# Moving key, value and chunk products of a hybrid encoder block into its scan, and re-ordering four waiting instructions

## The chip, the cores and the metric

One core of a Trainium2 chip runs the whole kernel in one launch. The metric is the device time of one execution in microseconds (us), as the median of the runs shown.

## The reference, cut to what matters

One layer on x of shape 1024 tokens x 1024 features, float32. A projection `z = rmsnorm(x) @ w_in` (4528 columns) feeds two branches:

```python
q = (rmsnorm(c_q) @ w_uq)                   # 8 heads, 64 plain + 32 rotary
kv = (rmsnorm(c_kv) @ w_ukv)                # 8 heads: k_nope (64), v_a (64)
o_a = softmax attention(q, [k_nope, k_rope], v_a)
q, k, v = silu(conv5(gdn_qkv))              # 4 heads of 128, q and k l2-normalised
o_b = delta rule scan, forward + backward   # state S_t per head, gated by g and beta
merged = sigmoid(gate_a) * (o_a @ w_proj_a) + sigmoid(gate_b) * (o_b @ w_proj_b)
x = x + merged @ w_out
x = x + square(relu(rmsnorm(x) @ w_ff1)) @ w_ff2
return rmsnorm(x)
```

`kv`, the products `q k^T` of the scan's chunks, the first projection, the second feed-forward product and the last norm are the places that the change touches.

## The kernel before, in words

Every matrix product in float32 precision is made of three passes of a reduced float32 form: each operand is split into a high part (a cast by ScalarE, ACT) and a low part (a subtraction by VectorE, DVE), and high x high, high x low and low x high are added up in PSUM (`mm3`, L158). Weights come through `wtile` (L143): a DMA on SyncE's queue (SP) into one of three `wraw` buffers, the cast (L147) and the subtraction (L149) into two of four `ws` buffers. One product with one input tile is 6 matmuls of 128x512. Tiles of 1024 columns come from two pools, `mem` (35 buffers) and `fill` (5 buffers); PSUM has two tiles of 1024 columns (`psA`) and four of 512 (`psB`). Within a program order that is set by the Python code, a list scheduler places each engine's instructions by its own model of the times; on the chip each engine then takes its queue strictly in that order, so an instruction that waits holds everything behind it on its engine.

The stages, with the times of the profiled execution:

- **Start (0 to about 40 us).** SP loads `w_in[0]`, eight tiles of x and, after the fourth, `w_in[1]` (L212 to L217). Each tile of x is scaled and cast on ACT (L233), its low part made on DVE (L234); the casts and low parts of the two weights are `wsplit` (L219; ACT L221, DVE L225), that of `w_in[1]` behind the fifth tile of x (L238). `z_pass` (L256, matmuls L258) goes through the tiles for both weights.
- **Projection stage (to 516 us).** The letters of the string `ORDER` (L45) say in which order the steps are emitted: `g` and `k`, `v`, `q` are tiles of the first projection (48 matmuls each, L156; DVE scales the result, L297), `s` and `i` the triangular solve (POOL masks it at L512, DVE works through it at L551 and L553), `c` the latent norms, `S` transposes, `Q` the attention queries, `z` the solve's products with chunks (transposes L693, L694). `K` (L622) makes keys of two heads: 6 matmuls, a scaled copy on ACT (L628) and a DMA to DRAM from ACT's queue (L629). `V` (L632) makes values of two blocks of 128 tokens: 3 matmuls each (L637), a copy on ACT (L639), a DMA from ACT's queue (L640). The weight of both, `wkv`, is loaded by the first `K`.
- **Chunk products (516 to 523 us).** `KQ` (L746): for four pairs of chunks, 8 products of 128x128 (each two instructions of the profile, L753) and one scaling on DVE (L756).
- **Scan (523 to 614 us).** Eight steps (L966), each for a forward and a backward chunk: `st_k` (L799 on PE, L801 on DVE), `st_v` (L810; DVE L815 makes R, ACT L818 copies vn), `st_s` (L828, DVE L832: the state), `st_o` (L845 with the state, L846 with vn; then ACT L849 or DVE L851). `scan_prep` of the next step is emitted after `st_v`: it loads a decay row (SP, L775, into a tile of `fill`), ACT L777, POOL L779 and L783, ACT L786, DVE L789. Step s uses chunk s forward and 7-s backward, so steps 0 and 1 need the pairs 0 and 3 alone, steps 2 to 5 the pairs 1 and 2. `load_v` reads the values back (SP L947, casts ACT L960, POOL and DVE L961); half of it is emitted in steps 3 and 4.
- **Attention (to 840 us), projections (to 1006 us), first feed-forward product (to 1316 us).** Untouched.
- **Second feed-forward product (1316 to 1591 us).** It begins with eight plain products (`plain_products` L1470: `mm3`, then DVE L1478 adds the result to Y), into which the weights of the first of 15 block products (`Visit`, L1108) are prepared: `blocks` (L1125) makes sums on DVE (L1128 to L1131) of the tiles that `load` (L1118, SP L1122) brings.
- **End (to 1654 us).** Four pieces of 256 tokens: 8 products (`piece` L1534), squares on ACT, sums on POOL and DVE, and `finish` (L1523), which norms the piece before, two of the eight tiles (DVE L1530, SP L1532) for each product of the next piece. The last piece is normed at L1578 to L1591.

Of the kernel before, what the change touches and what calls it, by code (L numbers as in the profile page):

```python
# [20 lines left out]
F32 = mybir.dt.float32  # L21
F32R = mybir.dt.float32r
I32 = mybir.dt.int32
AF = mybir.ActivationFunctionType
ALU = mybir.AluOpType
# [4 lines left out]
D = 1024  # L30
S = 1024
# [4 lines left out]
N = S // C  # L36
# [5 lines left out]

ORDER = "kkkmrvGGklGtvSvvGsciiSigiigcSSgiQigQQiiQgQgQigQgiQqgigoggiKVKVViKgigogigzzqggzqKqzggV"  # L45
PIECES = tuple((i, i + 256) for i in range(0, S, 256))
LEAD, LAG = 3, 2
VS, VS2 = (3, 4), (0, 1)
# [48 lines left out]
def block_kernel(ctx: ExitStack, tc: tile.TileContext, xT, pos, cpar, gpar, w_in, w_uq, w_ukv,  # L97
# [22 lines left out]
    def pb(name):  # L120
        return psB.tile([128, 512], F32, tag="B", name=name)
# [21 lines left out]
    def wtile(src, name):  # L143
        raw = wp.tile([128, 1024], F32, tag="wraw", name=f"{name}_r", bufs=3)
        nc.sync.dma_start(raw, src)
        hi = wp.tile([128, 1024], F32R, tag="ws", name=f"{name}_h", bufs=4)
        A.copy(hi, raw)  # L147
        lo = wp.tile([128, 1024], F32R, tag="ws", name=f"{name}_l", bufs=4)
        V.tensor_tensor(lo, raw, hi.bitcast(F32), ALU.subtract)  # L149
        return hi, lo  # L150
# [62 lines left out]
    for k in range(8):  # L213
        xt.append(mem.alloc())
        nc.sync.dma_start(xt[k].ap, xT[k * 128:(k + 1) * 128, :])
        if k == 3:
            w1 = wraw(w_in[1], "wi1")  # L217

    def wsplit(raw, name):  # L219
# [10 lines left out]
    for k in range(8):  # L230
        h, l = mem.pair()
        for sl in (HS if k < 2 else [slice(0, 1024)]):
            cast = A.activation(h.r[:, sl], xt[k].ap[:, sl], AF.Copy, scale=pcol(N1 + k))  # L233
            V.scalar_tensor_tensor(l.r[:, sl], xt[k].ap[:, sl], pcol(N1 + k), h.ap[:, sl],  # L234
                                   ALU.mult, ALU.subtract)
        xs.append((h, l))
        casts.append(cast)
        if k == 4:  # L238
            early.append(wsplit(w1, "wi1"))
    acc = fill.alloc()  # L240
    for k in range(8):
# [331 lines left out]
    lat = {}  # L573
# [46 lines left out]
                t.free()  # L620

    def s_K(h):  # L622
        if h == 0:
            wts["k"] = wtile(w_ukv, "wkv")
        psk = pa(f"ps_kk{h}")
        mm3(psk, wts["k"], h, [lat[1]])
        t = fill.alloc()
        A.mul(t.ap, psk, math.sqrt(SCALE))  # L628
        A.dma_start(d_k[h], t.ap)  # L629
        t.free()  # L630

    def s_V(i):  # L632
        for kb in (2 * i, 2 * i + 1):
            ks = slice(kb * 128, (kb + 1) * 128)
            psv = pb(f"ps_vv{kb}")
            for j, (a, b) in enumerate(((0, 0), (0, 1), (1, 0))):
                T.matmul(psv, lat[1][a].r[:, ks], wts["k"][b][:, 512:1024], start=j == 0, stop=j == 2)  # L637
            t = half("v")
            A.copy(t, psv)  # L639
            A.dma_start(d_v[kb], t)  # L640
        if i == 3:
            for t in lat[1]:
                t.free()


    d_gc = d_vl[3]
# [72 lines left out]
    def s_q(h):  # L719
# [1 line left out]
        late[0] = conv_tile(qT[h].ap, 12 + h, h)  # L721

    steps = {"k": s_k, "m": s_m, "l": s_l, "r": s_r, "G": s_G, "s": s_s, "t": s_t, "v": s_v,
             "S": s_S, "i": s_i, "g": s_g, "c": s_c, "Q": s_Q, "K": s_K, "V": s_V, "o": s_o,
             "z": s_z, "q": s_q}
    seen = dict.fromkeys(steps, 0)
    for c in ORDER:
# [15 lines left out]
        return lst[h].ap[:, n * C:(n + 1) * C]  # L743


    KQ = []  # L746
    for n2 in range(N // 2):
        psq = pa(f"ps_kq{n2}")
        for n in (2 * n2, 2 * n2 + 1):
            cs = slice(n * C, (n + 1) * C)  # L750
            for h in range(H):
                o = (n % 2) * 512 + h * 128
                T.matmul(psq[:, o:o + 128], kT[h].ap[:, cs], qT[h].ap[:, cs], start=True, stop=True)  # L753
        t = mem.alloc()
        rcol = st[:, i_r, 0:32].rearrange("p (h n) -> p n h", h=H)[:, 2 * n2:2 * n2 + 2, :]
        V.tensor_tensor(t.ap.rearrange("p (n h c) -> p n h c", n=2, h=H),  # L756
                        psq.rearrange("p (n h c) -> p n h c", n=2, h=H),
                        rcol.unsqueeze(3).to_broadcast([128, 2, H, C]), ALU.mult)
        KQ.append(t)


    OT = [mem.alloc().ap for _ in range(H)]
# [202 lines left out]
        scan_prep(0, d)  # L965
    for step in range(N):  # L966
        if step == N - 1:
            for t in KQ[::3] + KST:
                t.free()
        cc = []  # L970
        for d in range(2):
            n = step if d == 0 else N - 1 - step
            cc.append({"key": (step, d, n, slice(n * C, (n + 1) * C),
                               [d * 32 + h * N + n for h in range(H)])})
        for i, f in enumerate((st_k, st_v, st_s, st_o)):
            for c in cc:
                f(c)
            if i == 1 and step + 1 < N:
                for d in range(2):
                    scan_prep(step + 1, d)  # L980
            if i == 3 and step in VS:
                load_v(VS.index(step))
            if i == 3 and step + 2 == N:
                for t in KQ[1:3]:
                    t.free()
                for _ in load_head(0):
                    pass
            if i == 1 and step + 1 == N:
                for qb in range(LEAD):
                    attn_scores(0, qb)  # L990
                spill_q()
# [116 lines left out]
    class Visit:  # L1108


        def __init__(self, name, order, raw, xops, done):
            self.name, self.order, self.raw, self.xops, self.done = name, order, raw, xops, done
            self.g = len(xops)
            self.n = self.g * 128
            self.r = self.sums = self.banks = None
            self.w = {}

        def load(self):  # L1118
# [6 lines left out]
        def blocks(self):  # L1125
            (a11, a21), (a12, a22) = [(t[:, 0], t[:, 1]) for t in self.r]
            s3, s2, s1, s4 = (half(f"s{i}")[:, 0:self.n] for i in (3, 2, 1, 4))
            V.tensor_tensor(s3, a11, a21, ALU.subtract)  # L1128
            V.tensor_tensor(s2, a22, s3, ALU.subtract)
            V.tensor_tensor(s1, a21, a22, ALU.add)  # L1130
            V.tensor_tensor(s4, a12, s2, ALU.subtract)  # L1131
            self.sums = {1: a11, 2: a12, 3: s4, 4: a22, 5: s1, 6: s2, 7: s3}
# [115 lines left out]
    def run(visits, each):  # L1248
        seq = [(v, i) for v in visits for i in v.order]
        ahead = 3  # L1250
        for n in range(-ahead, len(seq)):
            if n + ahead < len(seq):
                v, i = seq[n + ahead]
                q = visits.index(v)
                if v.r is None:
                    v.load()
                if i == v.order[3] and q + 1 < len(visits):
                    visits[q + 1].load()
                v.prep(i)
            if n >= 0:  # L1260
                v, i = seq[n]
                each(v, i)
                v.product(i)
# [206 lines left out]
    def plain_products():  # L1470
        ul = ul0
        for mp in range(4):
            if mp < 3:
                w = wtile(w_ff2t[0, mp], f"w2_{mp}")
            for m in (2 * mp, 2 * mp + 1):
                ps = pa(f"ps_y{m}")
                mm3(ps, w if mp < 3 else [x.r for x in w3], m % 2 * 4, ul)
                V.tensor_tensor(Y[m], ps, Y[m], ALU.add)  # L1478
                if m == 7:
                    for t in w3 + [x for p in ul for x in p]:  # L1480
                        t.free()
                yield

    pp = plain_products()
    for m in range(6):
        next(pp)
# [12 lines left out]
    for q, (_, m, j0, j1) in enumerate(PLAN):  # L1499
        src = w_ff2[m].rearrange("p (a c) -> p a c", a=4)[:, :, j0 * 128:(j1 + 1) * 128]  # L1500
        v = Visit(f"y{q}", USUAL, [src[:, 0:2], src[:, 2:4]], Pairs(j0, j1), ff2_done(m))
        v.q = q
        vs.append(v)
    run(vs, each2)
    for j in UT:
        if j not in freed:
# [16 lines left out]
    def finish(sl, n):  # L1523
        ps = pb(f"ps_n3{n}")
        T.matmul(ps[:, 0:n], ones, xsq.ap[:, sl], start=True, stop=True)
        rsqrt(r3.ap[:, sl], ps[:, 0:n], 1.0 / D, eps_t[:, 0:1], half("m")[:, 0:n], half("t")[:, 0:n])
        for m in range(8):
            if m % 2 == 0:
                yield
            V.scalar_tensor_tensor(Y[m][:, sl], Y[m][:, sl], pcol(NF + m), r3.ap[:, sl],  # L1530
                                   ALU.mult, ALU.mult)
            nc.sync.dma_start(out[m * 128:(m + 1) * 128, sl], Y[m][:, sl])  # L1532
# [46 lines left out]
    T.matmul(psn, ones, xsq.ap[:, sl], start=True, stop=False)  # L1579
    T.matmul(psn, ones, sq, start=False, stop=True)  # L1580
    r, a_, b_ = r3.ap[:, sl], half("m")[:, 0:n], half("t")[:, 0:n]
    V.tensor_scalar(a_, psn, 1.0 / D, eps_t[:, 0:1], ALU.mult, ALU.add)
    A.activation(r, psn, AF.Ln, bias=eps_t[:, 0:1], scale=1.0 / D)
    A.activation(r, r, AF.Exp, scale=-0.5)
    A.activation(b_, r, AF.Square)
    V.scalar_tensor_tensor(b_, b_, -0.5, a_, ALU.mult, ALU.mult)
# [85 lines left out]
```

## Time and profile before

| what | value |
|---|---|
| median of 3 runs | 1654.64 us (1652.35 to 1661.54) |
| profiled execution, its own time | 1655.58 us |
| span of its profile | 1653.8 us |
| granted clock of TensorE, mean over the span | 0.987 |

The profiler's PE row is the matmuls, PEld the weight loads beside them. A wait is written "engine line <- what released it". "L156" is a line of the kernel, often that of a helper, so the tile names say which step it is.

### The profile page before, as it was taken

To read this page: it belongs to the slowest core of one execution; us is meant where nothing else is said; L and a number is where in the kernel's file an instruction comes from. 1 tells how busy PE (TensorE), PEld (TensorE's weight loads), DVE (VectorE), ACT (ScalarE), POOL (GpSimd) and SP (SyncE) were. 2 spreads that over 40 slices of the span, in tenths; PEclk is the share of its full clock that TensorE was granted. 3 is DMA by queue.
4 is the path that set the end of the run, shared out by engine and by line. 5 is a ranking of instruction groups with operands and counts; after the bars stand their busy time and mean duration, and the time that the engine had idled before them with its cause. 6 is when DMAs were issued, how large, how long until landed. Compare 5 with 4: busy or idle time off the path is not lost.

```text
span 1653.8 us, 21952 instructions
## 1 busy us (share of the span) xinstructions
PE 1601.6 (97%) x8235; PEld 1335.7 (81%) x8235; DVE 1213.9 (73%) x1781; ACT 790.7 (48%) x1360; POOL 257.0 (16%) x317
## 2 busy tenths in 40 slices
PE   7999999999999889999999999999999999999997
PEld 5787778877778887888878888888888877888796
DVE  5689899972444678888887668767776578887666
ACT  6456421442324558878762346444444533444333
POOL 0032300000002446555400000000000200111012
PEclk9999999999998999999999999999999999999998
DMA  5234243463224252111074211444333814444213
GB/s 198 75 100 112 102 153 115 133 206 107 76 91 157 45 169 90 39 39 39 5 250 153 102 51 54 169 152 154 140 148 139 292 58 149 161 151 144 83 58 103
DMA packets 83770, 197.01 MB, mean 119 GB/s; under 512 B 20160, under 2 KB 35648, under 8 KB 83408
## 3 DMA queue, kind: packets, MB, share of 16 engines
q1 hardware_dynamic: 51408, 127.34, 23.3%
q10 hardware_dynamic: 23600, 37.49, 6.3%
q0 software_dynamic: 8656, 30.78, 5.8%
q8 instruction: 65, 1.06, 0.3%
q14 instruction: 41, 0.34, 0.1%
HBM read 135.35 MB, written 60.23 MB: 118 GB/s over the span
## 4 chain that ended last, share of the span: by engine, by line
PE 73%; DVE 9%; DMA 4%; ACT 3%; POOL 2%; issue 2%; ACTq 0%; DVEq 0%; SPq 0%; POOLq 0%
PE ps_z L156 10%; PE ps_af L1151 10%; PE ps_ay L1151 7%; PE ps_w L156 5%; PE ps_p L156 5%; PE ps_cf L1151 5%; PE ps_s L881 5%; PE ps_pv L923 4%; PE ps_cy L1151 4%; PE ps_pt L904 3%; PE ps_df L1151 3%; PE ps_y L1540 2%; PE ps_y L156 2%; PE ps_dy L1151 2%; DMA f<-d_vl 2%
## 5 line engine op out<-in xcount | busy, mean ns | idle before, releaser
L156 PE MATMUL ps_z<-u,wi_h 128*128 128x512 f32 x1056 | 254.6, 397 | 6.4 <-DVE f L297 3.3
L156 PEld LDWEIGHTS ps_z<-u,wi_h 128*128 128x128 f32 x1056 | 199.4, 190 | 51.4 <-issue 5.2
L1151 PE MATMUL ps_af<-u,f_w 128*128 128x512 f32 x768 | 182.3, 390 | 0.0
L1151 PEld LDWEIGHTS ps_af<-u,f_w 128*128 128x128 f32 x768 | 144.0, 188 | 30.7 <-issue 0.5
L1151 PE MATMUL ps_ay<-u,y_w 128*128 128x512 f32 x576 | 138.8, 390 | 1.9 <-DVE YB L1418 1.2
L156 PE MATMUL ps_z<-u,wi_l 128*128 128x512 f32 x528 | 129.8, 396 | 0.0
L1151 PEld LDWEIGHTS ps_ay<-u,y_w 128*128 128x128 f32 x576 | 107.6, 188 | 25.8 <-ACT y_w L1139 1.9
L156 PEld LDWEIGHTS ps_z<-u,wi_l 128*128 128x128 f32 x528 | 99.7, 190 | 21.1
L881 PE MATMUL ps_s<-u,u 128*128 128x512 f32 x384 | 105.0, 406 | 2.1 <-POOL u L870 1.4
L884 DVE TENSOR_REDUCE sx<-ps_s 128x1 f32<-128x1024 f32 x64 | 78.0, 1219 | 19.7 <-PE ps_s L881 17.6
L1151 PE MATMUL ps_cf<-u,f_w 128*128 128x512 f32 x384 | 92.3, 389 | 0.0
L886 ACT ACTIVATE u<-ps_s,sx 128x1024 f32<-128x1024 f32 x64 | 72.3, 1130 | 32.1 <-DVE sx L884 31.7
L910 DVE TENSOR_TENSOR u<-ps_pt,u 128x512 fp32r<-128x512 f32 x128 | 82.4, 680 | 5.1 <-ACT u L909 5.1
L888 POOL TENSOR_SCALAR u<-u,sx 128x1024 f32<-128x1024 f32 x64 | 72.2, 1131 | 84.8 <-DVE sx L887 82.0
L1151 PEld LDWEIGHTS ps_cf<-u,f_w 128*128 128x128 f32 x384 | 72.1, 188 | 15.0
L1275 POOL DMA_DIRECT2D u<-d_u x16 | 8.7, 547 | 484.4 <-DMA w_r<-w_ff2t 472.2
L881 PEld LDWEIGHTS ps_s<-u,u 128*128 128x128 f32 x384 | 67.5, 189 | 14.3 <-POOL u L870 2.2
L147 ACT CAST wi_h<-wi_r 128x1024 fp32r<-128x1024 f32 x34 | 35.8, 1052 | 89.6 <-PE ps_z L156 82.8
L297 DVE TENSOR_TENSOR f<-ps_z,u 128x1024 f32<-128x1024 f32 (+1 forms) x36 | 41.7, 1160 | 48.4 <-PE ps_z L156 48.3
L1140 DVE TENSOR_TENSOR f_w<-f_r,f_w 128x512 fp32r<-128x512 f32 x48 | 33.1, 690 | 55.8 <-ACT f_w L1139 55.8
L309 DVE SCALAR_TENSOR_TENSOR u<-f,par,u 128x1022 f32<-128x1022 f32 (+1 forms) x48 | 64.6, 1363 | 12.7 <-ACT u L305 12.0
L1292 ACT ACTIVATE u<-u 128x512 f32<-128x512 f32 x64 | 40.5, 633 | 65.4 <-DVE u L1291 64.4
(408 smaller groups left out, 3388.3 us busy)
## 6 DMA issues: line engine op xcount, KB each, us to landing
wi_r<-w_in SPq DMA_DIRECT2D x36, 512.0 KB, 4.4
u<-d_u POOLq DMA_DIRECT2D x36, 512.0 KB, 4.0
f_r<-w_ff SPq DMA_DIRECT2D x32, 512.0 KB, 3.2
d_u<-u SPq DMA_DIRECT2D x24, 512.0 KB, 3.5
d_z<-f ACTq DMA_DIRECT2D x20, 512.0 KB, 4.7
f<-d_z SPq DMA_DIRECT2D x20, 512.0 KB, 3.9
y_r<-w_ff SPq DMA_DIRECT2D x18, 512.0 KB, 4.6
d_u<-u ACTq DMA_DIRECT2D x16, 512.0 KB, 2.6
```

Of the source, the lines that this page charges most:

```text
L156: T.matmul(ps[:, sl], w, x[:, sl], start=start, stop=stop)
L297: V.tensor_tensor(dst[:, sl], ps, r1.ap[:, sl], ALU.mult)
L309: V.scalar_tensor_tensor(dst[:, d0:d1], z[:, d0 + o:d1 + o], pcol(c + t), dst[:, d0:d1], ALU.mult, ALU.add)
L881: T.matmul(pss[:, sl], a.r[:, qsl], b.r[:, sl], start=i == 0, stop=i == 2)
L884: V.tensor_reduce(sx[:, 0:1], pss, AX.X, ALU.max, negate=True)
L886: A.activation(P.ap, pss, AF.Exp, bias=sx[:, 0:1], accum_out=sx[:, 1:2])
L888: G.tensor_scalar(P.ap, P.ap, sx[:, 1:2], 1.0, ALU.mult, ALU.mult)
L904: T.transpose(pt[:, k * 128:(k + 1) * 128], P.ap[:, ko:ko + 128], ident)
L910: V.tensor_tensor(lv, p3, hf_, ALU.subtract)
L923: T.matmul(pso[:, 0:256], VC[kb].r[:, h * 128:(h + 1) * 128], PT[kg][i].r[:, k * 256:(k + 1) * 256], start=kb == 0 and i == 0, stop=kb == ...
L1151: T.matmul(ps, w[:, a, k * 128:(k + 1) * 128], self.xops[k][i].parts[b], start=n == 0 and i in FIRST, stop=n == 3 * self.g - 1, skip_group ...
L1292: A.activation(t, t, AF.Square)
```

## The change

The letters `K` and `V` leave `ORDER`, and a `g` and an `S` move ahead of the first `i`. The first and the last pair of `KQ` are made before the scan; the pairs 1 and 2, the four `V` and the four `K` become entries of a table, `fillers`, which the scan's loop calls after a given part of a given step. `s_V` takes its PSUM from `psA`. `w_in[1]` is loaded after the first tile of x and split behind the first tile's cast. The first instruction of the first `blocks` is ordered behind the fourth addition of the plain products. `finish` pauses at tiles 0, 3 and 6 in place of 0, 2, 4 and 6. In the last norm ACT's Ln is emitted ahead of DVE's scaling.

```diff
-ORDER = "kkkmrvGGklGtvSvvGsciiSigiigcSSgiQigQQiiQgQgQigQgiQqgigoggiKVKVViKgigogigzzqggzqKqzggV"
+ORDER = "kkkmrvGGklGtvSvvGscSgiiigiigcSSgiQigQQiiQgQgQigQgiQqgigoggiiigogigzzqggzqqzgg"
...
-        if k == 3:
+        if k == 0:
             w1 = wraw(w_in[1], "wi1")
...
-        if k == 4:
+        if k == 0:
             early.append(wsplit(w1, "wi1"))
...
     def s_K(h):
-        if h == 0:
-            wts["k"] = wtile(w_ukv, "wkv")
         psk = pa(f"ps_kk{h}")
...
     def s_V(i):
...
-            psv = pb(f"ps_vv{kb}")
+            psv = psA.tile([128, 512], F32, tag="A", name=f"ps_vv{kb}")
...
-        if i == 3:
-            for t in lat[1]:
-                t.free()
...
-    KQ = []
-    for n2 in range(N // 2):
+    KQ = {}
+
+    def chunk_kq(n2):
         psq = pa(f"ps_kq{n2}")
...
-        KQ.append(t)
+        KQ[n2] = t
+
+    fillers = {(0, 0): (chunk_kq, 1), (0, 1): (chunk_kq, 2), (0, 2): (s_V, 0), (0, 3): (s_V, 1),
+               (1, 1): (s_V, 2), (1, 3): (s_V, 3), (2, 1): (s_K, 0), (3, 1): (s_K, 1),
+               (4, 1): (s_K, 2), (5, 1): (s_K, 3)}
+    chunk_kq(0)
+    chunk_kq(3)
+    wts["k"] = wtile(w_ukv, "wkv")
...
         for i, f in enumerate((st_k, st_v, st_s, st_o)):
             for c in cc:
                 f(c)
+            if (step, i) in fillers:
+                g, k = fillers.pop((step, i))
+                g(k)
+                if not fillers:
+                    for t in lat[1]:
+                        t.free()
...
     def blocks(self):
...
-            V.tensor_tensor(s3, a11, a21, ALU.subtract)
+            ins = V.tensor_tensor(s3, a11, a21, ALU.subtract)
+            if self.after is not None:
+                tc.add_manual_dep(ins.ins, self.after.ins.name, nosync, reason="order")
...
-                V.tensor_tensor(Y[m], ps, Y[m], ALU.add)
+                added.append(V.tensor_tensor(Y[m], ps, Y[m], ALU.add))
...
+    vs[0].after = added[3]
     run(vs, each2)
...
-            if m % 2 == 0:
+            if m % 3 == 0:
                 yield
...
+    A.activation(r, psn, AF.Ln, bias=eps_t[:, 0:1], scale=1.0 / D)
     V.tensor_scalar(a_, psn, 1.0 / D, eps_t[:, 0:1], ALU.mult, ALU.add)
-    A.activation(r, psn, AF.Ln, bias=eps_t[:, 0:1], scale=1.0 / D)
```

## Rows read from the trace of the kernel before

**Rows 1.** Busy time by stage: PE, PEld, DVE, ACT, POOL, granted clock, DMA share, GB/s
```profile
0.00:216.00 216.00, 199.31 (x895) 158.85 (x896) 168.32 (x215) 120.27 (x206) 42.05 (x45) 0.99 0.36 115
216.00:350.00 134.00, 132.76 (x583) 108.66 (x582) 130.33 (x126) 41.83 (x39) 0.99 (x2) 1.00 0.39 131
350.00:516.00 166.00, 164.20 (x971) 129.36 (x970) 63.81 (x69) 47.32 (x59) 5.05 (x9) 0.95 0.42 132
...
526.00:606.00 80.00, 68.25 (x540) 65.99 (x539) 53.38 (x159) 43.87 (x125) 38.64 (x70) 0.94 0.31 86
...
360.00:380.00 20.00, 20.00 (x90) 16.57 (x89) 4.71 (x4) 4.24 (x4) 2.92 (x6) 1.00 0.77 202
```

**Rows 2.** Waits of the scan, 526 to 606: total us, times, longest
```profile
ACT f L777 <- DMA f<-d_vl: 14.7, 6, 4.4
PE ps_o L846 <- ACT u L818: 11.2, 7, 2.5
```

**Rows 3.** The scan's first step, ACT's timeline: start, length, what, idle before
```profile
527.67 0.63 ACT L777 ACTIVATE f<-f 128x512 f32<-128x512 f32 x1 [4.37 <-DMA f<-d_vl]
528.21 0.57 ACT L818 COPY u<-ps_v 128x512 f32<-128x512 f32 x1
```

**Rows 4.** The chain of waits in order of time: one projection tile of 48 matmuls
```profile
248.85 10.88 PE ps_z L156 x48
```

**Rows 5.** Timeline at the chunk products
```profile
515.80 7.34 PEld L753 LDWEIGHTS ps_kq<-u,u 128*128 128x128 f32 x64
516.03 7.30 PE L753 MATMUL ps_kq<-u,u 128*128 128x128 f32 x64
516.22 0.33 ACTq L640 DMA_DIRECT2D d_v<-v  x1
```

**Rows 6.** Instructions by tile (ps_kk, ps_vv, vr): ns min/median/max, first and last start
```profile
L628 ACT ACTIVATE f<-ps_kk x4: 1007/1028/1034, 348.5 to 469.7; 128x1024 f32<-128x1024 f32 x4
L639 ACT COPY v<-ps_vv x8: 567/588/595, 349.9 to 517.6; 128x512 f32<-128x512 f32 x8
L960 ACT CAST vc<-vr x6: 387/404/408, 507.3 to 515.2; 128x256 fp32r<-128x256 f32 x6
```

**Rows 7.** DMA issues: size and median us to landing
```profile
d_v<-v ACTq DMA_DIRECT2D x8, 256.0 KB, 4.9
vr<-d_v SPq DMA_DIRECT2D x4, 512.0 KB, 5.7
```

**Rows 8.** Timeline of the start
```profile
8.38 6.86 PE L258 MATMUL ps_z<-u,wi_h 128*128 128x512 f32 x16 [8.38 <-ACT u L233]
15.60 1.03 ACT L221 CAST wi_h<-wi_r 128x1024 fp32r<-128x1024 f32 x1
16.69 10.74 PE L258 MATMUL ps_z<-u,wi_h 128*128 128x512 f32 x46 [0.21 <-ACT wi_h L221]
18.06 3.67 DVE L234 SCALAR_TENSOR_TENSOR u<-u,par,u 128x1024 fp32r<-128x1024 f32 x3
```

**Rows 9.** Timeline of 160 to 190, POOL, DVE and PE
```profile
162.50 16.80 POOL L512 TENSOR_SCALAR_AFFINE_SELECT SY<-SY 128x1024 f32<-128x1024 f32 x4 [20.76 <-DVE SY L511]
...
179.34 0.27 DVE L551 TENSOR_TENSOR f<-SY 128x62 f32<-128x62 f32 x1 [4.34 <-POOL SY L512]
...
183.46 6.86 PE L156 MATMUL ps_z<-u,wi_h 128*128 128x512 f32 x22 [2.79 <-DVE f L297]
```

**Rows 10.** The solve's last DVE step and the first product that needs it (chain of waits)
```profile
345.09 0.70 DVE SY L553
...
401.31 1.07 PE ptx L694 x16
```

**Rows 11.** Waits of 1318 to 1328
```profile
DVE s L1128 <- DMA y_r<-w_ff: 7.6, 1, 7.6
...
PE ps_y L156 <- DVE YB L1478: 2.8, 1, 2.8
```

**Rows 12.** Timeline of the end
```profile
1641.54 1.01 DVE L1530 SCALAR_TENSOR_TENSOR f<-f,par,u 128x256 f32<-128x256 f32 x2
...
1644.61 0.48 DVE L1582 TENSOR_SCALAR m<-ps_n,eps_t 128x256 f32<-128x256 f32 x1 [1.39 <-PE ps_n L1580]
1645.13 0.47 ACT L1583 ACTIVATE u<-ps_n,eps_t 128x256 f32<-128x256 f32 x1 [1.00 <-DVE m L1582]
```

More of the change, by code (lines that the diff above doesn't have):

```diff
@@ L723, in block_kernel @@
     steps = {"k": s_k, "m": s_m, "l": s_l, "r": s_r, "G": s_G, "s": s_s, "t": s_t, "v": s_v,
-             "S": s_S, "i": s_i, "g": s_g, "c": s_c, "Q": s_Q, "K": s_K, "V": s_V, "o": s_o,
+             "S": s_S, "i": s_i, "g": s_g, "c": s_c, "Q": s_Q, "o": s_o,
              "z": s_z, "q": s_q}
@@ L967, in block_kernel @@
         if step == N - 1:
-            for t in KQ[::3] + KST:
+            for t in [KQ[0], KQ[3]] + KST:
                 t.free()
@@ L983, in block_kernel @@
             if i == 3 and step + 2 == N:
-                for t in KQ[1:3]:
+                for t in (KQ[1], KQ[2]):
                     t.free()
@@ L1114, in __init__ @@
             self.n = self.g * 128
-            self.r = self.sums = self.banks = None
+            self.r = self.sums = self.banks = self.after = None
             self.w = {}
@@ L1482, in plain_products @@
                 yield
+    added = []
     pp = plain_products()
```

## The prediction

> **What bounds the kernel now.** I read the busy times by stage first, because a share over the whole span hides where TensorE (PE) waits. Up to 216 us PE is idle for 16.7 us (216 - 199.31), most of it before its first matmul at 8.38 [rows 1, 8]. From 216 to 516 it is idle for 1.24 + 1.80 = 3.0 us of 300: these stages are bound by the number of matmuls, and each one taken out shortens them. In the scan, 526 to 606, it is idle for 11.75 us of 80, and its granted clock averages 0.94, so some of that stage runs at 1.2 instead of 2.4 GHz [rows 1].
>
> The waits of the scan say why. Seven times, 11.2 us in all, PE's L846 waits for ACT's copy L818; ACT in turn stands in L777 for the DMA of a decay row, 14.7 us in six waits [rows 2]. The first step shows the order: L777 waits 4.37 us for its DMA and L818 follows it in the same queue, although its own input is older [rows 3]. So once a step PE has nothing to do, about 1.45 us ((11.2 - 2.5) / 6) and 2.5 us in the first step. That hole is what the change wants to fill. The other waits it touches are single: PE's slow first matmuls [rows 8], 2.79 us behind DVE at 183 [rows 9], 2.8 us at 1324 [rows 11], and the last norm [rows 12].
>
> **The change, part by part** (against the profiled execution's own 1655.58 us, 0.94 us above the median shown; that difference is within the runs' spread, so I make no correction for it).
>
> *K and V out of the projection stage.* Four K of 6 matmuls and eight blocks of V of 3 are 48 matmuls of 128x512; a projection tile of 48 took 10.88 us [rows 4]. PE is the bound there, so -10.9 us. Their copies on ACT and DMAs leave that stage too, which is worth nothing there: ACT is busy for 47 of 166 us after 350 [rows 1]. The pairs 1 and 2 of the chunk products, 32 of the 64 instructions or 3.65 us [rows 5], only move from just before the scan into its first step: no change in work.
>
> *The same work in the scan.* Step 0 gets the two pairs and two V (2.72 us) and has a wait of 2.5 us: 0. Step 1 gets two V, 2.72 us, against 1.45: +1.3. Steps 2 to 5 get a K each, 6 x 0.2267 = 1.36 us against 1.45: PE has room, but ACT, which causes the wait, also gets the copy (1.03 us) and the issue of the DMA (0.33) [rows 5, 6]; I take +0.3 a step, +1.2. The six casts of values that ran before the scan, 6 x 0.40 = 2.4 us [rows 6], now cannot start until the new V are in DRAM and read back; about two of five hit a queue in front of L818: +1.0. Sum **+3.5**. Also new on ACT's queue are 8 copies and 8 issues of V, and the cast of `wkv`; on SP's queue the load of `wkv` and two loads of values now stand among the decay loads (L775), and a load of values waits until its d_v has landed (4.9 us) and takes 5.7 [rows 7]; they are emitted three steps after the writes, so I cost that at nothing. The K's tile takes the fifth `fill` buffer, so a decay load starts later by up to one part of a step; a tile is loaded more than a step before `st_o` needs it. Bounds: -2 (all the work goes into idle time, 10.9 of 11.75, and the lower clock goes with the holes) and, were everything added to ACT to lie ahead of L818, +27 (below).
>
> *First weights earlier.* Now PE takes 16 matmuls in 6.86 us, with one weight alone, and then 46 in 10.74, when the second weight's cast (15.60 + 1.03) is done: the first pass ends at 27.4 [rows 8]. With the second weight behind the first tile of x, each tile brings 8 matmuls, 1.81 us, and PE falls behind the arrivals soon. At best 64 x 0.2267 = 14.5 us from 8.38, 22.9; DVE's last low part (18.06 + 3.67 = 21.7) and four matmuls after it, 22.6, allow that. But the load moves past three tiles of x on SP, the first tile's matmuls wait for the cast, and DVE gets the low part of the weight earlier. I let PE be paced by its own work from the second tile on: 24.4, **-3.0**; bounds 0 (each tile of x one transfer later) and -4.5.
>
> *S and g ahead of i.* POOL masks until 179.3, DVE stands 4.34 us in the first L551, and behind it in DVE's queue is the L297 for which PE waits 2.79 us [rows 9]. With a projection tile and the transposes emitted first, DVE and PE have work that does not need the mask. I take **-2.0**, bounds 0 and -2.8; next late is then DVE, which is busy for 130 of 134 us after 216 [rows 1].
>
> *Feed-forward start.* DVE's first sum waits 7.6 us for its tile; the addition L1478 stands behind it, and PE's next PSUM tile behind that: 2.8 us [rows 11]. Ordered behind the fourth addition, the sum waits for nothing, for its DMA is long there. The sums are used after the sixth of the eight plain products, two products or 2 x 24 x 0.2267 = 10.9 us behind the fourth. **-2.7**, bounds 0 and -2.8.
>
> *Last norms.* ACT's Ln waits 1.00 us for DVE's scaling of the same PSUM tile, 0.48 us of it the scaling itself [rows 12]; with Ln first the scaling moves beside ACT's next two: **-0.4**, bounds 0 and -0.5. Pausing `finish` at every third tile takes the last pair of L1530 (1.01 us at 1641.54) from between the last additions and puts it ahead of them; DVE has the same work before the last square either way: **0**, bounds +0.5 and -0.5.
>
> Sum: -10.9 + 3.5 - 3.0 - 2.0 - 2.7 - 0.4 = -15.5; 1655.6 - 15.5 = **1640**. All best bounds together: 1655.6 - 10.9 - 2 - 4.5 - 2.8 - 2.8 - 0.5 - 0.5 = 1631.6.
>
> **The rivals.**
>
> *The scan has no room.* Then its 10.9 us of new matmuls lengthen it by 10.9, not 3.5: 1640 + 7.4 = 1647.5. For it: the weight loads fill 65.99 of 80 us, 82%, and in a projection tile, where PE never stops, they fill 16.57 of 20, 83% [rows 1]. Against it: in the scan all matmuls are 128 columns wide, and in the chunk products, of that width and without a stop, 64 loads span 7.34 us, as long as the matmuls themselves [rows 5], so 82% leaves some 14 us free. The Trainium skill (Perfetto Trace Analysis, "Identifying the Most-Contended Engine") calls matmul busy time a bad measure and asks for LDWEIGHTS busy % instead. By that measure taken across stages the scan would be as full as a projection tile and this rival's time would hold; the trace agrees only as long as the width of the matmuls is not looked at.
>
> *ACT and SP become the scan's bound (slower).* ACT gets 8 x 0.59 + 4 x 1.03 of copies, 12 x 0.33 of issues, 2.4 of casts and 1.0 for `wkv`, 16.2 us [rows 5, 6, 8], and its queue is what delays L818 now. If all of it falls ahead of L818, and one read of values stands on SP and ACT from its write on (4.9 + 5.7 = 10.6 us [rows 7], with the decay loads behind it), the scan grows by 26.8: 1655.6 - 10.9 + 26.8 - 8.1 = 1663.4. It turns to slower at 19 us. Against it: ACT is busy for 43.87 of 80 us [rows 1], and most additions come where it stands waiting.
>
> *The solve comes late.* The last step of the solve on DVE ends at 345.8 and its first user on PE is at 401.3 [rows 10]. Of these 55 us of cover, six K and V (8.2 us) and one projection tile (10.9) go, since a `g` moved forward; 36 us remain for DRAM write, read and the queues between. If they are too few PE waits for the difference; with 8 us, 1648.
>
> *The change doesn't do what it says.* The order of emission is only a wish to the scheduler, and x may come as late as the second weight came early: without the gains of the start and of S and g, 1645.
>
> **How the numbers follow.** My forecast 0.60; no room 0.17; solve late 0.08; no effect of the two orders 0.08; slower 0.07. Some 0.5% (8.3 us, below 1646.4) is what a measurement of this kernel can tell from no change. Nearly all of the forecast (0.58), most of the fourth case (0.06), a third of the second (0.06) and of the third (0.03) lie below it: faster 0.73. The rest of these, and part of the last, lie within: same 0.21; slower 0.06. The range, 1631 to 1650, begins at the sum of the best bounds and takes in the rivals at 1645 to 1648; what is left out is the slower case and the tails.
>
> **What would show it.** Right: the projection stage ends some 16 us earlier with PE as full as now; between L818 and L846 little of the 11.2 us is left, and ps_kk and ps_vv stand in its place; the scan from its first st_v to its last st_o is 2 to 8 us longer including the two chunk pairs; PE's first pass ends near 24; the waits at 183 and 1324 are gone. Wrong: a new wait of L846 on L818 of over 2 us a step, waits of ACT's L960 or SP's L775 on d_v, or PE waiting for f<-d_x before the first ptx.

## The result and the profile after

| kernel | median of its runs | ratio to the kernel before, 95% interval |
|---|---|---|
| changed | 1635.98 us (1634.11 to 1636.78, 4 runs) | 0.9873 [0.9855, 0.9892] |
| changed, measured again beside other runs | 1636.73 us (4 runs) | 0.9875 [0.9859, 0.9891] |

The kernel before stood at 1655.69 beside the first of these. The change makes the kernel faster by 1.3%, 19.7 us; the forecast was 1640, faster. The profiled execution of the changed kernel took 1634.11 us with a span of 1632.4, so the two traces differ by 21.4 us of span. Lines of the changed kernel are a little higher: the copy of vn is L822 (before: L818), its user L850 (L846), the exponential of the decay row L781 (L777), the decay load L779 (L775).

Where TensorE (PE) waits now, over the whole span (engine line, what it waited for, total us, times, longest):

```profile
PE ps_z L258 <- ACT u L233: 8.4, 1, 8.4
PE ps_ck L586 <- ACT q L585: 4.3, 1, 4.3
PE ps_v L814 <- DVE u L805: 3.0, 1, 3.0
PE ps_z L156 <- DVE u L297: 2.6, 1, 2.6
PE ps_n L1593 <- DVE u L1586: 2.4, 1, 2.4
...
PE ps_o L850 <- ACT u L822: 1.7, 1, 1.7
```

Of the 11.2 us for vn's copy [rows 2] only 1.7 are left, and the 2.79 us at 183 [rows 9] and the 2.8 us at 1324 [rows 11] are gone. Two waits stand in their place: 4.3 us at ps_ck, where 1.2 us had been, and 3.0 us at ps_v in the scan. The stages answer to [rows 1], here the last part of the projection stage and the scan, from the first chunk product to the last ps_o (PE, PEld, DVE, ACT, POOL busy, granted clock, DMA share, GB/s):

```profile
390.30:496.10 105.80, 105.80 (x736) 82.39 (x736) 44.08 (x40) 30.44 (x35) 0.00 (x0) 0.97 0.30 96
496.10:597.60 101.50, 93.83 (x724) 87.95 (x724) 67.53 (x178) 64.30 (x161) 47.97 (x82) 0.98 0.49 152
```

The same stretch of the kernel before, cut at the same two instructions:

```profile
516.00:613.90 97.90, 85.91 (x676) 82.63 (x675) 65.34 (x176) 54.40 (x145) 45.62 (x80) 0.95 0.39 110
```

So the chunk products begin 19.9 us earlier (516.0 to 496.1) and the scan, now with K and V, is 3.6 us longer. PE never stops in the 105.8 us ahead of the scan. Another 4.8 us go in the eight plain products of the second feed-forward product, where the wait of [rows 11] was, and the rest is unchanged to within 0.4 us.

**The granted clock** is part of it. Behind some of its longer waits PE runs on at half clock for a while. The wait at ps_ck shows it, in rows of 2 us (columns as above):

```profile
206.00:208.00 2.00, 0.00 (x0) 0.00 (x0) 1.97 (x4) 0.00 (x0) 0.00 (x0) 1.00 0.00 0
208.00:210.00 2.00, 1.20 (x2) 0.69 (x3) 2.00 (x4) 1.87 (x3) 0.00 (x0) 0.66 0.00 0
210.00:212.00 2.00, 2.00 (x5) 0.82 (x3) 1.93 (x4) 0.56 (x1) 0.00 (x0) 0.50 0.44 111
```

The granted clock falls to 0.50 (1.2 of 2.4 GHz) just when PE has work again: 5 matmuls in 2 us, where a full projection tile has 9. One such stretch costs 1.7 us. I summed 2 us times (1 - granted clock) over all such rows of a clock below 0.97 from 30 to 1340 us: 17.0 us in the profiled execution of the kernel before (ten of these stretches), 8.5 in the changed one (five). So up to 8.5 of the 21.4 us are clock. The same sum stands in the table below for each experiment, as "lower clock".

Not all of it hangs on waits. In the changed kernel three of the five stretches lie behind the waits of 2.6, 4.3 and 3.0 us above, but the two at 410 and 447 us lie in the 105.8 us in which PE does not stop, right behind transposes of 64x64 (ptz). In the kernel before 8.5 of the 17.0 us lie between 408 and 498 us, where no wait is longer than 1.1 us, and behind its own wait of 2.60 us, which ends at 75.5, the clock does not fall. What decides it is open. The sums are also of one execution each: the profiled one of the changed kernel has a mean granted clock of 0.993, its other three 0.988 to 0.990.

### The profile page after: what moved, and what is told of

The parts are those of the page before. It is cut to its first block, busy times and chain, and to the rows that moved or that the text cites. A ratio compares the mean times of both kernels' runs of the same rounds, so it can differ in the third digit from the quotient of the medians.

```text
span 1632.4 us, 21964 instructions
## 1 busy us (share of the span) xinstructions
PE 1590.9 (97%) x8235; PEld 1329.9 (81%) x8235; DVE 1216.8 (75%) x1781; ACT 791.9 (49%) x1361; POOL 254.5 (16%) x317
## 4 chain that ended last, share of the span: by engine, by line
PE 79%; DVE 7%; DMA 2%; ACT 2%; issue 1%; POOL 1%; SPq 0%; DVEq 0%; ACTq 0%; POOLq 0%
PE ps_z L156 15%; PE ps_af L1163 11%; PE ps_ay L1163 7%; PE ps_cf L1163 5%; PE ps_w L156 5%; PE ps_p L156 5%; PE ps_s L885 5%; PE ps_pv L927 4%; PE ps_cy L1163 4%; PE ps_pt L908 3%; PE ps_df L1163 3%; PE ps_y L156 3%; PE ps_y L1554 2%; PE ps_dy L1163 2%; DMA f<-d_vl 1%
## 5 line engine op out<-in xcount | busy, mean ns | idle before, releaser
L309 DVE SCALAR_TENSOR_TENSOR u<-f,par,u 128x1022 f32<-128x1022 f32 (+1 forms) x48 | 64.6, 1362 | 11.8 <-ACT u L305 11.1
L1163 PE MATMUL ps_cy<-u,y_w 128*128 128x512 f32 x288 | 70.6, 389 | 0.3 <-DVE f L1430 0.3
```

Of the source, the lines that this page charges most:

```text
L309: V.scalar_tensor_tensor(dst[:, d0:d1], z[:, d0 + o:d1 + o], pcol(c + t), dst[:, d0:d1], ALU.mult, ALU.add)
L1163: T.matmul(ps, w[:, a, k * 128:(k + 1) * 128], self.xops[k][i].parts[b], start=n == 0 and i in FIRST, stop=n == 3 * self.g - 1, skip_group ...
```

## The experiments

Each edit is to the changed kernel, if nothing else is said. "Scan" is first chunk product to last ps_o in the profiled execution.

| run | median us | ratio to before, interval | first chunk product at | scan | lower clock |
|---|---|---|---|---|---|
| before | 1654.5 to 1657.0 | | 516.0 | 97.9 | 17.0 |
| changed | 1636.0, 1636.7 | 0.9873, 0.9875 | 496.1 | 101.5 | 8.5 |
| e1 feed-forward order undone | 1640.6 | 0.9914 [0.9900, 0.9928] | 495.9 | 101.1 | 10.3 |
| e2 first weights undone | 1639.1 | 0.9909 [0.9896, 0.9923] | 500.2 | 101.7 | 11.9 |
| e3 S and g undone | 1642.4 | 0.9924 [0.9909, 0.9939] | 500.3 | 101.5 | 12.0 |
| e4 K and V undone | 1640.4 | 0.9922 [0.9906, 0.9937] | 509.7 | 92.4 | 10.2 |
| e6 K, V without matmuls | 1627.1 | 0.9818 [0.9804, 0.9832] | 499.0 | 91.2 | 15.3 |
| e7 values after decay rows | 1630.7 | 0.9845 [0.9829, 0.9861] | 496.2 | 98.1 | 8.5 |
| e8 norm split | 1636.9 | 0.9882 [0.9866, 0.9899] | 501.1 | 102.9 | 17.1 |
| e9 before, copies first | 1649.2 | 0.9954 [0.9937, 0.9970] | 516.3 | 93.1 | 13.6 |
| e10 = e4, copies first | 1639.4 | 0.9894 [0.9876, 0.9912] | 508.0 | 91.7 | 8.5 |
| e11 low parts on POOL | 1642.1 | 0.9908 [0.9888, 0.9927] | 500.0 | 98.8 | 10.3 |
| e12 norm's tile first | 1623.9 | 0.9828 [0.9801, 0.9855] | 487.8 | 99.2 | 3.3 |

The intervals are mostly about 2.5 us to each side (4.5 for e12), so a single part of 2 to 6 us is measured to half its size at best. Medians and ratios differ by as much: e1 to e4 stand 4.7, 3.1, 6.4 and 4.4 us above the changed kernel by the medians, 6.8, 6.0, 8.4 and 8.1 by the ratios, and 3.9, 4.9, 5.0 and 4.7 by the spans of the profiled executions. The landmarks of the traces are finer, where the lower clock is set apart.

**One part undone at a time.** The feed-forward start first.

```diff
-    vs[0].after = added[3]
```

> The changed kernel with one line taken out: the first sum of the first blocks (DVE L1138) is no longer ordered behind the fourth addition of the plain products. Theory A (a wait of PE costs its own length and the lower granted clock of the matmuls that follow it): the wait of some 2.8 us between the fourth and the sixth plain product is back, the 16 matmuls behind it take 5.3 us in place of 3.6, and the time is 4.8 us above the changed kernel's 1636.0, 1640.8. Theory B (as the sum on record has it, the wait alone): +2.7, 1638.7. In the trace A wants a stretch of half clock right behind the wait; B wants none.

Theory A holds: 4.7 us above the changed kernel by the medians. PE's rows in this run show the wait and what follows it (start, length, work, idle before):

```profile
1304.99 1.97 PE L156 MATMUL ps_y<-u,w_l 128*128 128x512 f32 x8
1309.57 5.54 PE L156 MATMUL ps_y<-u,w_h 128*128 128x512 f32 x16 [2.60 <-DVE YB L1490]
```

and the same two rows of the changed kernel:

```profile
1305.69 1.98 PE L156 MATMUL ps_y<-u,w_l 128*128 128x512 f32 x8
1307.50 3.79 PE L156 MATMUL ps_y<-u,w_h 128*128 128x512 f32 x16
```

The wait is 2.60 us and the 16 matmuls behind it take 5.54 in place of 3.79: 1.75 us more, which a row of waits does not hold.

```diff
-        if k == 0:
+        if k == 3:
             w1 = wraw(w_in[1], "wi1")
...
-        if k == 0:
+        if k == 4:
             early.append(wsplit(w1, "wi1"))
```

> The changed kernel with the second weight loaded behind the fourth tile of x and split behind the fifth, as before the change. Theory A (the start's gain is given back at the next place where PE waits for DVE): the first pass ends some 1.4 us later, near 27.3 us, and the time is within 1 us of the changed kernel's 1636.0. Theory B (the term on record): +3.0, 1639.0.

Theory B is nearer: 3.1 us above by the medians. My reason for A fell too: ps_n1a starts 1.31 us later than in the changed kernel (34.48 against 33.17) and ps_ck still 1.27 later (210.07 against 208.80), so what the start gains is kept. Of the 4.9 us between the two spans 1.3 are this; nearly all the rest is lower clock (11.9 against 8.5 us), half of it behind no wait, so whether it belongs to the order is open.

```diff
-ORDER = "kkkmrvGGklGtvSvvGscSgiiigiigcSSgiQigQQiiQgQgQigQgiQqgigoggiiigogigzzqggzqqzgg"
+ORDER = "kkkmrvGGklGtvSvvGsciiSigiigcSSgiQigQQiiQgQgQigQgiQqgigoggiigigogigzzqggzqqzgg"
```

> The changed kernel with S and g back behind the first two i, as before the change. Theory A (the reordering only moved a wait from 183 us, 2.79 us, to ps_ck at 208 us, 4.33 us): the two waits of 2.8 and 1.2 us are back, the one of 4.3 is gone, and the time is within 1.5 us of the changed kernel's 1636.0. Theory B (the term on record): +2.0, 1638.0.

Both miss: 6.4 us above. The waits came out as A says:

```profile
183.07 9.09 PE L156 MATMUL ps_z<-u,wi_h 128*128 128x512 f32 x32 [2.76 <-DVE f L297]
...
198.79 1.98 PE L586 MATMUL ps_ck<-q,ones 128*128 128x512 f32 x4 [1.25 <-ACT q L585]
```

2.76 + 1.25 = 4.0 us of waits against 4.33, but the first transposes of the solve (ptz) come 1.2 us later than in the changed kernel, although this execution began 0.65 earlier, and from there to the chunk products it loses 3.0 us more (108.8 against 105.8) at a clock of 0.94 against 0.97 (lower clock 12.0 against 8.5). So in the traces some 1.8 of the 5.0 us are order and the rest is clock, behind no wait; whether that clock belongs to the order is open.

```diff
-ORDER = "kkkmrvGGklGtvSvvGscSgiiigiigcSSgiQigQQiiQgQgQigQgiQqgigoggiiigogigzzqggzqqzgg"
+ORDER = "kkkmrvGGklGtvSvvGscSgiiigiigcSSgiQigQQiiQgQgQigQgiQqgigoggiKVKVViKgigogigzzqggzqKqzggV"
...
-    fillers = {(0, 0): (chunk_kq, 1), (0, 1): (chunk_kq, 2), (0, 2): (s_V, 0), (0, 3): (s_V, 1),
-               (1, 1): (s_V, 2), (1, 3): (s_V, 3), (2, 1): (s_K, 0), (3, 1): (s_K, 1),
-               (4, 1): (s_K, 2), (5, 1): (s_K, 3)}
+    fillers = {(0, 0): (chunk_kq, 1), (0, 1): (chunk_kq, 2)}
```

> The changed kernel with K and V back in the projection stage, at their old places and with wkv loaded by the first K; the two chunk pairs stay in the scan's first step. Theory B (the terms on record: 10.9 us of matmuls out of one stage, 3.5 us into the other): +7.4, 1643.4. Theory A (the stage lost more than its 48 matmuls, since the projection stage from 120 us on came out 20.2 us shorter and the scan only 3.6 us longer; waits and stretches of lower clock went with the K and V): +9 to +13, 1645 to 1649. If the scan had no room: 0, 1636.

By the medians neither: 4.4 us above, less than the 7.4 on record, which the ratios (8.1) do not exclude. The stage behaves as A has it, 13.6 us longer (10.9 of matmuls, 1.7 of lower clock, the rest small waits). The scan is 9.1 us shorter without K and V, where the record had 3.5. The four parts undone give 4.7 + 3.1 + 6.4 + 4.4 = 18.6 us by the medians, 18.5 by the spans, about the whole change; by the ratios they give 29, so the single sizes are rough.

**What K and V cost in the scan.** Then I left out the matmuls alone.

```diff
-            psv = psA.tile([128, 512], F32, tag="A", name=f"ps_vv{kb}")
-            for j, (a, b) in enumerate(((0, 0), (0, 1), (1, 0))):
-                T.matmul(psv, lat[1][a].r[:, ks], wts["k"][b][:, 512:1024], start=j == 0, stop=j == 2)
             t = half("v")
-            A.copy(t, psv)
+            A.copy(t, lat[1][0].ap[:, 0:512])
...
-        psk = pa(f"ps_kk{h}")
-        mm3(psk, wts["k"], h, [lat[1]])
...
-        A.mul(t.ap, psk, math.sqrt(SCALE))
+        A.mul(t.ap, lat[1][0].ap, math.sqrt(SCALE))
```

> The changed kernel itself once more, beside the runs of this group, so that they have a common measure: within 1.5 us of its 1636.0 by every theory. In the first group, where one part was undone at a time, the medians stood 4.7 (feed-forward start), 3.1 (first weights), 6.4 (S and g) and 4.4 us (K and V) above 1636.0, 18.6 in all.

> The changed kernel with the 48 matmuls of K and V left out: ACT copies a stretch of the latent tile instead, and the copies and DMAs stay as they are (so attention works on other keys and values). It asks what PE's part of the fillers costs in the scan. Theory A (the scan had room for a third of them: with K and V in the stage the scan takes 92.4 us from the first chunk product to its last ps_o, in the changed kernel 101.5, 1.7 of them lower clock): 7 us less than the changed kernel, 1629, and the waits of ps_o for ACT's copy of vn back at 7 to 9 us. Theory B (the term on record): 3.5 us less, 1632.5. Theory C (not the matmuls but the copies and DMAs on ACT and SP cost the time): 0 to 2 us less.

The changed kernel repeats. Without the matmuls the time is 9.6 us lower and the scan 10.3 us shorter: more than A, and its second half fails. The waits for vn's copy did not come back. The scan of e4 (columns as in the stages above) and its longest sum of waits:

```profile
509.70:602.10 92.40, 81.30 (x676) 78.19 (x676) 65.53 (x176) 54.25 (x145) 45.53 (x80) 1.00 0.40 117
```

```profile
PE ps_o L852 <- ACT u L824: 9.0, 6, 2.5
```

and the same two views of e6:

```profile
499.00:590.20 91.20, 84.72 (x676) 81.19 (x675) 67.44 (x179) 63.72 (x161) 46.87 (x82) 0.96 0.54 165
```

```profile
PE ps_o L845 <- ACT u L817: 3.2, 1, 3.2
```

In e6 PE has nothing to put into the holes, yet it is idle for 6.5 us, not for 12.0 as before. So holes closed that no matmul of K and V filled. The lower clock has a part too: 5.1 us of it lie in the scan before, none in e4, 3.4 in e6. So e4 is already 5.5 us shorter than the scan before, though 9.0 us of its waits for vn's copy are left. ACT's queue shows what differs between e4 and e6. In e4, as before the change [rows 3], a step reads: exponential of the decay row, which waits for its DMA, then the copies of vn (L824):

```profile
536.62 0.63 ACT L783 ACTIVATE f<-f 128x512 f32<-128x512 f32 x1 [2.52 <-DMA f<-d_vl]
...
539.22 0.61 ACT L783 ACTIVATE f<-f 128x512 f32<-128x512 f32 x1
539.74 0.56 ACT L824 COPY u<-ps_v 128x512 f32<-128x512 f32 x1
```

In e6 (and in the changed kernel) the copies come first:

```profile
535.43 0.59 ACT L817 COPY u<-ps_v 128x512 f32<-128x512 f32 x1 [0.81 <-DVE u L814]
536.26 0.59 ACT L817 COPY u<-ps_v 128x512 f32<-128x512 f32 x1 [0.24 <-DVE u L814]
536.74 1.15 ACT L776 ACTIVATE f<-f 128x512 f32<-128x512 f32 x2
```

Before, and in e4 from its second step on, the exponentials of the next step stand first; with K and V in the scan (or only their copies and DMAs) the copies stand first or between them in all steps but two. The scheduler turned the order round; by which of the new instructions is open. The next two runs test the order alone:

```diff
-        A.copy(c["vn"], pv)
+        copies[d] = A.copy(c["vn"], pv)
...
-            A.activation(qs, ar, AF.Exp)
+            ins = A.activation(qs, ar, AF.Exp)
+            for x in copies.values():
+                tc.add_manual_dep(ins.ins, x.ins.name, nosync, reason="order")
```

> The kernel before, with one order added and nothing else: in each step of the scan ACT's L777 of the next step (which waits for the DMA of a decay row) comes behind the two copies of vn (L818). Theory A (the holes of the scan were made by the order of ACT's queue alone; K and V did not fill them, their presence only turned that order round): the 11.2 us in which ps_o waits for L818 fall below 4, PE's idle time in the scan from 12.0 to 6 or 7 us, and the time by 5 to 9 us (the upper end with the lower clock of that stretch gone too), to 1648 to 1652 beside a kernel before of about 1656. Theory B (the decay row is on the critical path itself, so that its DMA's wait moves to another place): 0 to -2.

> The changed kernel with K and V back in the projection stage (as in e4_KV_in_stage, 1640.4) and the same order added: ACT's exponential of the decay row behind the step's two copies of vn. Theory A (K and V cost their full 10.3 to 10.9 us of matmuls in either stage, and all that their move brought was the order on ACT): the scan falls from 92.4 to 86 to 88 us, the wait of 9.0 us below 4, and the time is that of the changed kernel or less, 1634 to 1636. Theory B (the holes can only be used by putting work in them): 1640.

e9 has the time that A wants: the kernel before gains 6.7 us by the medians from this order alone, and the waits for vn's copy leave the list. But PE's idle time falls only to 93.10 - 83.37 = 9.7 us, not to 6 or 7. The scan, and its waits:

```profile
516.30:609.40 93.10, 83.37 (x676) 79.19 (x675) 65.08 (x177) 55.32 (x146) 44.34 (x80) 1.00 0.40 116
```

```profile
PE ps_v L812 <- DVE u L803: 2.7, 3, 1.0
PE ps_o L847 <- DVE u L853: 2.5, 4, 1.0
PE ps_o L847 <- ACT u L851: 2.0, 1, 2.0
```

The gain lies in the first step. From the first chunk product to the second step's first ps_k the kernel before takes 18.2 us and e9 12.9: the wait of 2.5 us ahead of ps_o at 528.9 and the 3.4 us of lower clock behind it are gone. From there to the last step's first ps_k it is 66.9 against 65.7 us: in these steps the holes of 1.0 to 1.5 us mostly come back as waits for DVE, so there the wait only moves, as in B.

e10 misses: 1639.4, a scan of 91.7 and not 86 to 88, for short waits on DVE (4.2 and 2.5 us) take the place of the 9.0. The first step had nothing left to give: in e4 its copies no longer stand behind its exponentials, and e4 and e10 both take 12.5 us to the second step's first ps_k. Against e10, K and V in the scan are worth 2.3 us (spans 1634.7 and 1632.4, both with 8.5 us of lower clock) to 3 (medians); with the loads of values put right as well (e7, below) it is 5.8 (spans) to 8.7 (medians).

**The new wait in the scan.** In the changed kernel SP's queue reads:

```profile
513.50 16.14 SPq L951 DMA_DIRECT2D vr<-d_v  x3
529.69 20.33 SPq L779 DMA_DIRECT2D f<-d_vl  x6
```

The third load of values stands until 529.3, about when its d_v, issued at 524 to 525, has landed by [rows 7]; the decay loads stand behind it, ACT's L781 then waits for them, and DVE's L805 behind that.

```diff
+        tc.add_manual_dep(ins.ins, decay[0].ins.name, nosync, reason="order")
```

(`ins` is the load of values L951, `decay[0]` the decay load emitted last.)

> The changed kernel with each load of values (SP L951) ordered behind the decay load (SP L779) that was emitted last before it. Theory A (SP stands at a load of values until its d_v has landed, at 529.3 us, and step 3's decay loads stand behind it, so that ACT L781, DVE L793 and DVE L805 come late and PE waits 3.0 us at ps_v): that wait and the 1.7 us of lower clock behind it go, 1631.5. Theory B (the decay loads wait for a fill buffer that the K's tile holds): the wait stays, 1636. Either may lose a little at the start of attention, where the values now come later.

A, without its second half: 6.0 us below the changed kernel, the scan 3.4 us shorter. SP's queue, then ACT's waits on the decay rows (7.1 us, 4 times, in the changed kernel):

```profile
502.22 32.50 SPq L779 DMA_DIRECT2D f<-d_vl  x6
534.82 0.45 SPq L951 DMA_DIRECT2D vr<-d_v  x1
```

```profile
ACT f L781 <- DMA f<-d_vl: 3.1, 2, 1.7
```

The lower clock is 8.5 us in both, and the spans differ by 3.5 us, so the trace bears 3.5 of the 6.0; the rest is not settled.

**The wait at ps_ck.** Two ways to close it, and one through POOL:

```diff
-ORDER = "kkkmrvGGklGtvSvvGscSgiiigiigcSSgiQigQQiiQgQgQigQgiQqgigoggiiigogigzzqggzqqzgg"
+ORDER = "kkkmrvGGklGtvSvvGscSgiiigiicgcSSgiQigQQiiQgQgQigQgiQqgigoggiiigogigzzqggzqqzgg"
...
-        else:
-            lat[1] = lora_norm(11, 1, 128, KVN, "ps_ck")[0]
+        elif i == 1:
+            wts["z"] = lora_z(11, 1)
+        else:
+            lat[1] = lora_norm(11, 1, 128, KVN, "ps_ck", wts["z"])[0]
```

> The changed kernel with the second latent norm in two parts, its projection tile first, then a g, then the squares and ps_ck (the g before it moves behind the tile). Theory A (PE waits 4.33 us at ps_ck for DVE's L297, which stands in the solve's queue, and has only 1.9 us of transposes to do meanwhile): with 10.9 us of a projection tile in between the wait and the 1.7 us of lower clock behind it go, 1630 to 1631.7. Theory B (DVE is the bound of this stretch, busy for 95.4 of 102.5 us before 223 and 76.0 of 77 behind it): the same wait turns up at the next user of DVE's results, 1635 to 1636.

B: the wait turns into 3.8 us for L297 and 1.9 us for ps_q, and nothing is gained. (The profiled execution takes 1641.3 us, 4.4 above the median, with 17.1 us of lower clock.) Then, with e7's order:

```diff
-            w = wtile(w_in[i], f"wi{i}")
+            w = wtile(w_in[i], f"wi{i}", G if i in (6, 18, 11, 19) else V)
```

> The changed kernel with the loads of values behind the decay loads (e7_values_after_decay, 1630.7), and the low parts of four weights (tiles 6, 18, 11 and 19 of the first projection, L149) made on POOL instead of DVE: POOL is idle there, and DVE holds up PE for 2.6 us at 74 and for 4.3 us at 208 behind its queue. Theory A (each L149 of 1.2 us that leaves DVE's queue lets L297 start that much earlier): the wait at 208 falls from 4.3 to about 0.7, that at 74 from 2.6 to about 1.3, and with one or two stretches of lower clock less the time is 5 to 8 us below e7, 1623 to 1626. Theory B (DVE stays the bound of the stretch from 170 to 300, as in e8_norm_split, or POOL is too slow for the low parts and PE waits for them): 1630 or more.

A failure: 11 us above e7 by the medians, 5.7 by the spans, with 11.1 us of wait at ps_ck. POOL's low part and DVE's row beside it:

```profile
181.52 2.99 POOL L149 TENSOR_TENSOR wi_l<-wi_r,wi_h 128x1024 fp32r<-128x1024 f32 x1 [3.87 <-ACT wi_h L147]
```

```profile
182.17 2.48 DVE L553 TENSOR_TENSOR SY<-SY,f 128x122 f32<-128x122 f32 x1
```

and the same DVE instruction in the changed kernel:

```profile
183.54 0.29 DVE L553 TENSOR_TENSOR SY<-SY,f 128x122 f32<-128x122 f32 x1
```

DVE stood still until POOL was done, three times in that stretch, and L297 of the norm's tile came behind two more steps of the solve than before. Last, with e7's order, the place in DVE's queue alone:

```diff
+            if i == 11:
+                tc.add_manual_dep(tps[1].ins, ins.ins.name, nosync, reason="order")
```

(`ins` is L297 of the norm's tile, `tps[1]` the first instruction of the solve's thirteenth step.)

> The changed kernel with the loads of values behind the decay loads (e7_values_after_decay, 1630.7), and in the solve's DVE queue one step of L551 (the one of 128x650, at 201.5 us) ordered behind the L297 of the second latent norm's tile, for which PE waits 4.3 us at ps_ck. DVE then stands about 1 us until PE has made that tile, at 202.6 us. Theory A (only the place in the queue is wrong; DVE's work has 45 us of cover until the solve's first user): the wait at ps_ck falls below 0.5 us, the lower clock behind it goes, and the time is 4 to 6 us below e7, 1625 to 1627. Theory B (DVE is the bound of the stretch to 300 us, as e8_norm_split looked): the wait comes back at the next tiles and the time is 1630 to 1631.

A, and a little more by the medians: 1623.9, 6.8 us below e7 and 1.7% below the kernel before, the fastest of those that do the whole work. By the ratios (0.9845 and 0.9828) it is 2.8 us, with intervals that overlap.

```profile
199.94 0.80 DVE L557 TENSOR_TENSOR SY<-SY,f 128x612 f32<-128x612 f32 x1
201.80 1.91 PE L331 MATMUL ps_st<-ident,u 128*128 128x128 f32 x16
202.00 1.23 DVE L297 TENSOR_TENSOR f<-ps_z,u 128x1024 f32<-128x1024 f32 x1 [1.26 <-PE ps_z L156]
...
203.94 1.98 PE L590 MATMUL ps_ck<-q,ones 128*128 128x512 f32 x4 [0.23 <-ACT q L589]
```

DVE stands 1.26 us so that PE need not stand 4.3. ps_ck comes 4.9 us earlier than in e7, in which the start has 0.7; the solve still has cover. Only 3.3 us of lower clock are left, against 8.5; of the difference 1.7 us lay behind the wait, the 3.4 at 410 and 447 us behind none. Two of the five runs of e12 take 1628.9 and 1631.6 us, at a mean granted clock of 0.991 in place of 0.995. So the 4.1 us of wait are shown to be the order's, the rest is not.

## Why the prediction was right, and where its terms were not

Sign, range and size held: 1640 forecast, 1636 measured, inside 1631 to 1650. The sum held because errors of its terms went both ways; that it came so close is in part luck.

- *K and V out of the projection stage, -10.9.* Right for the matmuls; e4 shows 13.6 in that stage, with 1.7 of lower clock and small waits, which I left out.
- *The same work in the scan, +3.5.* The number fits (+3.6), its reason fell. "That hole is what the change wants to fill" was the failing step: without the matmuls of K and V the scan is 6.7 us shorter than before (97.9 to 91.2), and the matmuls then cost 10.3 (91.2 to 101.5), nearly all of their 10.9; e7 makes it 6.9. Against e4, whose later steps keep the old order, it is 9.1 and 5.7. So in the changed kernel the rival without room was nearer to the mechanism. Of the 6.7 us that paid for it e9 shows 4.8 by the order of ACT's queue alone, which I had read in [rows 3] and taken as fixed: the first step's wait and the lower clock behind it, for which my sum had no term. The other 1.9 us are not taken apart. The Trainium skill (Perfetto Trace Analysis, "Identifying the Most-Contended Engine") asks for LDWEIGHTS busy % in place of matmul busy time. Taken across stages, a reading that I had set aside, 82% made the scan full; the price in e6 agrees with that reading, and with the loads of values put right (e7) only in part.
- *First weights, -3.0.* Undone, 3.1 by the medians. But the first pass ends at 26.1, not at 24.4: its 64 matmuls take 17.70 us, not 14.5, so PE is not paced by its own work from the second tile on. The trace keeps 1.3 us; the rest, as far as the trace shows it, is lower clock.
- *S and g, -2.0.* Mis-sized: 6.4 undone by the medians; 1.8 of the 5.0 us between the spans are order. The wait at 183 is gone as I said, and I named DVE as next late, but not where: at ps_ck, 4.33 us. e12 shows what lay there.
- *Feed-forward start, -2.7.* The wait was right (2.60 in e1); the term was too small by the lower clock behind it: 4.5 us between the traces, 4.7 by the medians.
- *Last norms, -0.4, and the pauses, 0.* From the last ps_n to the end 8.75 us against 9.22: -0.5. Ahead of ps_n PE now waits 2.4 us for DVE where it waited 1.9; from the end of the last product it is 12.3 us against 12.7, so -0.4 for both.
- *Rivals.* The solve does not come late: the 1.1 us in which the kernel before waited for f<-d_x are gone. That the orders do nothing fell with e1 to e3. The slower one had its place right, a load of values on SP ahead of the decay loads; its price was 3 to 6 us, not 26.8. I had put it at nothing because the loads are emitted three steps after the writes; on SP's queue the first three start at 513.5, 518.6 and 529.3 us, among writes issued from 508.8 to 525.3.

## What to carry to other kernels

Before you put work into a hole, ask whether the hole is only an order: look at what stands ahead of the late instruction in its engine's queue, and move that. Then look whether the step got shorter: in e9 the first step did, by 5.3 us, while in the six behind it most of the holes came back behind another engine. A wait can cost more than its length: behind most of the waits of 2.4 to 4.3 us here came a stretch of half clock, 1.7 us and more. Where an engine is busy throughout, one of its instructions may still hold up another engine by its place in the queue; letting it stand 1.3 us took 4.1 us of wait away.

## What was not expected of the hardware

- The lower clock alone was 17.0 us of the profiled execution before, 8.5 after, 3.3 in e12, and the difference that no wait explains in e2 and e3 goes with it. Half of it before, and 3.4 us after, came behind no wait.
- In e11 a subtraction of 128x1024 on POOL (2.4 to 3.0 us) held a two-input instruction of DVE until it was done: 0.29 us became 2.48. The Trainium skill (GPSIMD Engine Reference, "1. Specifications") says that POOL shares its SBUF interfaces with VectorE and contends with DVE instructions that have two SBUF inputs; the trace of e11 agrees.
